# Gates on ScalarE and a later modulation row in a two-block transformer kernel

## The chip, the cores and the metric

The kernel runs on one core of a Trainium2 chip. The core has five engines with queues of their own, which work in order and wait for each other by semaphores: TensorE (PE in the profile; its weight loads are PEld), VectorE (DVE), ScalarE (ACT), GpSimd (POOL) and SyncE (SP), which here only issues transfers. POOL issues transfers too, among them the indirect gathers. The metric is the device time of one execution in microseconds (us); what is compared is the median over several executions.

## The reference, cut to what matters

Two transformer blocks work on 256 tokens of width 1024, all in float32. The first has three attentions, a gated merge and a sparse feed-forward (PEER): for each token, 8 heads pick 16 of 16384 experts each, and an expert is one row `u` and one row `v`.

```python
act = gelu(einsum('chkd,cd->chk', u[ic], hc))      # 128 picks for each token
w = gate * act
out = einsum('chk,chkd->cd', w, v[ic])
```

The second block has two layers, each with a mixer and an expert-choice MoE, on the tokens ("latents") and, in the first layer, on a context of 256 tokens. All norms of it are modulated by rows that come from a condition vector: `mod = silu(c) @ ada_w[i] + ada_b[i]`, cut in six rows of 1024 (shift, scale and gate of the mixer, then of the MoE). The mixer of the first layer is an mLSTM, whose output is normed by head and gated:

```python
y = y * rsqrt(mean(y * y, -1) + EPS)
y = y.reshape(b, t, h * d) * norm_g * sigmoid(o)
```

The mixer of the second layer is a retention.

## The kernel before, in words

The program is one straight line of instructions, written by Python generators that are woven into each other: `drive` runs a main generator and lets side generators go on in proportion to costs that the generators yield. From this the framework makes each engine's order: it simulates the program and places, on each engine, what is ready, with preference by the written order. So the order of an engine's queue isn't exactly the written one, and an edit at one place can move others.

Memory is handed out by hand: an arena `fa` in SBUF, two rings `rt` and `rw` for rounded halves of operands, and eight PSUM banks (`pp`). Weights come as slabs of 1 MB through `Stream`: a dry run records the order of all requests, and in the real run a slab is issued from SP, in that order, as soon as one of some four slots is free. Most weights are split into two parts (high and low, `Units`): ACT copies with rounding, DVE or POOL subtracts; a product is then three matmuls.

First block (0 to some 411 us): projections, attentions and merge, limited by PE. Beside them, `ada_task` (L1222) computes rows of the modulation: for each row it loads the bias, asks for four slabs of `ada_w`, runs 32 small matmuls, and `ada_put` (L1217) adds the bias on DVE and writes the row to DRAM by a transfer from POOL, twice (latents and context). Before, eight rows are done there, two of them of the second layer, and what is left of the last is finished at the start of `peer` (L1276).

`peer` (L1274) norms the tokens, and `mod_cols` (L1512) brings shift and scale of several norms from DRAM as columns: small transfers from POOL, one transpose on PE, copies and fused products on DVE. L1280 does it for the first layer, L1281 for the second layer's mixer.

Then the picks (`picks`, L1332) run as main generator, and beside them, as side work, the query products and routing (`prepare` L1293, `prepare_last`, `route`) and the whole first mixer of the context (`context_task` L1590). Tokens lie on the 128 partitions, in two tiles; for each tile there are 128 picks, one column of the `act` and `gate` arrays each. One pick is: POOL gathers one row of `u` and `v` for each token (1 MB) into one of eight ring buffers; DVE multiplies `u` by the token and sums along the row into a column of `act`; ACT applies Gelu to the column; DVE multiplies it by the gate's column (L1364); ACT makes a diagonal matrix of it by scaling the identity (L1368); PE multiplies this by `v` and adds up in PSUM. A buffer goes back to the ring when PE has read it. The first picks wait for the routing of the first head, which is some 60 instructions of DVE.

The mLSTM: `mlstm_attend` computes head after head, and `mlstm_norm` (L1880), woven beside it, computes the output gates: four products of 512 columns for each of context and latents, each made into a sigmoid by an Exp on ACT, an addition and a reciprocal on DVE (L1888 to L1891). When two heads are there, `norm_pair` (L1906) multiplies them by the inverse root mean square (three Newton steps on DVE) and by the gate. It also serves the retention. Context: beside the picks; latents: after the picks, `mlstm` (L1603).

Then come the first MoE, the retention and the second MoE. The MoEs stream expert weights and are close to what the transfers can do. `block2` (L1536) hands `moe` a function `late` (L1547) that is called when the last group's up-projection is done; it gets room for what the retention needs. The retention starts with norms that use the columns of the second layer's first rows.

Of the kernel before, what the change touches and what calls it, by code (L numbers as in the profile page):

```python
# [14 lines left out]
AF = mybir.ActivationFunctionType  # L15
OP = mybir.AluOpType
AX = mybir.AxisListType

EPS = 1e-6
# [3 lines left out]
RING, BATCH = 8, 1  # L23
# [490 lines left out]
class K:  # L514
# [323 lines left out]
    def block1(self, mem):  # L838
        mT = self.norm_T([m.a for m in mem], self.col("g_mem"), w=1024)
        for m in mem:  # L840
            m.free()
        self.ada_open()
        self.ada = self.ada_task([(0, k) for k in range(6)] + [(1, 0), (1, 1)])
        self.hT = self.norm_T([x.a for x in self.x], self.col("g_mix"))
        self.mkv = self.f(2048)

        mkv = self.mkv.v("p (i f) -> p i f", i=2)
        for s in range(2):
            for i, p in enumerate(self.wide([mT], self.halves("w1", 2 * s))[0]):
                self.act(mkv[:, i, s * 512:(s + 1) * 512], p.a)  # L850
                p.free()
        for b in mT:
            b.free()
        self.dil_buffers()
        self.drive(self.proj_task(), [self.mem_task(), self.sb_task(), self.dil_task()], 0.6)
        self.merge_task()
# [417 lines left out]
    def peer(self):  # L1274
        h2, g = [self.f(1024, True), self.f(1024)], self.bcast_row("ffn")
        self.ada_steps(99)  # L1276
        self.mc = self.f(128, True)
        h2T = self.norm_T([x.a for x in self.x], self.col("g_ffn"), sums=self.sq.a[:, :4], rows=(g, h2))
        self.sq.free(), g.free()
        self.mod_cols(0, [(n, b) for n in range(2) for b in range(2)])  # L1280
        self.mod_cols(1, [(0, 0), (1, 0)])  # L1281
        self.routes = [{"heads": 0, "rows": self.f(128), "gate": self.f(128), "act": self.f(128)} for _ in range(2)]

        for i, x in enumerate(self.x):
            self.nc.sync.dma_start(self.keep[i], x.a)
            x.free()
        self.nc.sync.dma_start(self.keep[2], h2[1].a)
        h2[1].free()
        side = self.chain((0.3 * c for c in self.prepare(h2T)), self.weave(self.context_task(), [self.prepare_last()], 1.5))
        self.drive(self.picks(h2, side), [side], PACE)  # L1290
        self.stream.grow(1)

    def prepare(self, h2T):  # L1293

        self.sc = [self.plain(self.RA) for _ in range(2)]
        sub = self.stream.get(("w1", W1["sub"]))
        self.units.lo = deque([self.nc.gpsimd])
        for s in range(8):
            w = self.wslab(("w1", W1["pq"] + s))
            p = self.slab_T(h2T, w)  # L1300
            q = self.f(512)
            self.act(q.a, p.a)
            p.free()
            self.wfree(w)
            p = self.ps()
            for i in range(2):
                for f in range(2):
                    self.mm(p.a[:, i * 256 + f * 128:i * 256 + f * 128 + 128], q.a[:, f * 256 + i * 128:f * 256 + i * 128 + 128],
                            sub.a[:, (2 * s + f) * 128:(2 * s + f + 1) * 128])
            for i in range(2):  # L1310
                self.act(self.sc[i].a[:, s * 256:(s + 1) * 256], p.a[:, i * 256:(i + 1) * 256])
            p.free(), q.free()
            yield 5200
            if s == 1:
                self.units.lo = deque([None, self.nc.gpsimd])
            if s == 7:
                for b in h2T:
                    b.free()
                sub.free()
                self.stream.shrink(2)  # L1320
                self.units.lo = deque([None])
            if s in (0, 1, 3, 7):
                yield from self.route(0, {0: 0, 1: 1, 3: 2, 7: 4}[s], s + 1)
# [8 lines left out]
    def picks(self, h2, prep):  # L1332


        ident = self.c("ident")
        ring = dg = None
        for i, r in enumerate(self.routes):
            while r["heads"] < 1:
                yield next(prep) * 0
            if ring is None:  # L1340
                ring, dg = deque(self.f(2048, True) for _ in range(RING)), deque(self.f(128, True) for _ in range(4))
            if i:
                self.nc.sync.dma_start(h2[0].a, self.keep[2])
            po = self.ps(2)
            rows, gate, act = (r[n].a for n in ("rows", "gate", "act"))
            for k in range(0, 128, BATCH):
                while r["heads"] * 16 < k + 1:
                    yield next(prep) * 0
                if i and k == 128 - BATCH:

                    ring.popleft().free()
                    self.x = [self.f(1024) for _ in range(2)]
                    self.nc.sync.dma_start(self.x[0].a, self.keep[0])
                got = []
                for j in range(k, k + BATCH):
                    b = ring[0].a
                    ring.rotate(-1)
                    got.append(b)
                    self.nc.gpsimd.indirect_dma_start(b, None, self.t["puv"], bass.IndirectOffsetOnAxis(ap=rows.bitcast(U32)[:, j:j + 1], axis=0))  # L1359
                    self.stt(b[:, :1024], b[:, :1024], 1.0, h2[0].a, OP.mult, OP.mult, accum_out=act[:, j:j + 1])  # L1360
                    yield 2600
                o = act[:, k:k + BATCH]
                self.act(o, o, AF.Gelu)
                self.tt(o, o, gate[:, k:k + BATCH], OP.mult)  # L1364
                for j, b in enumerate(got):
                    d = dg[0].a
                    dg.rotate(-1)
                    self.act(d, ident, AF.Copy, scale=act[:, k + j:k + j + 1])  # L1368
                    for f in range(2):
                        self.mm(po.a[:, f * 512:(f + 1) * 512], d, b[:, 1024 + f * 512:1024 + (f + 1) * 512], k + j == 0, k + j == 127)  # L1370
            if i == 0:
                x = ring[0].a[:, :1024]
                ring.rotate(-1)
            else:
                x = self.x[1].a
            self.nc.sync.dma_start(x, self.keep[i])
            for f in range(2):
                o = x[:, f * 512:(f + 1) * 512]
                self.tt(o, po.a[:, f * 512:(f + 1) * 512], o, OP.add)
            if i == 0:  # L1380
                self.nc.sync.dma_start(self.keep[0], x)
            po.free()
            for n in ("rows", "gate", "act"):
                r[n].free()
        h2[0].free()
        for b in (*ring, *dg):
            b.free()
# [148 lines left out]
    def block2(self, upto):  # L1536
# [10 lines left out]
        def late():  # L1547
            self.sq = self.f(16)
            junk.extend(self.f(256) for _ in range(2))
            self.ret_open()  # L1550

        def squares(n, k):
# [28 lines left out]
        s, r = self.root_mean([x.a for x in self.x], late[1].a[:, :8])  # L1581
# [298 lines left out]
    def mlstm_norm(self, S):  # L1880

        S["yT"] = self.r(2048), self.r(2048)
        for s in range(2):

            b = self.f(1024)
            for i, p in enumerate(self.wide([S["hT"]], self.halves("w2", 8 + 2 * s, S["seg"]))[0]):
                o = b.a[:, i * 512:(i + 1) * 512]
                self.act(o, p.a, AF.Exp, scale=-1.0)  # L1888
                p.free()
                self.ts(o, o, 1.0, OP.add)  # L1890
                self.nc.vector.reciprocal(o, o)  # L1891
            if s == 1:
                for x in S["hT"]:
                    x.free()
            yield 9800
            for j in (4 * s, 4 * s + 2):
                while S.get("heads", 0) < j + 2:
                    yield 5200
                self.norm_pair(S["y"], b, 512, j % 4 * 128, S["ss"].a[:, :16].rearrange("p (i h) -> p i h", i=2)[:, :, j:j + 2], j)
                self.pair_T(S["yT"], [S["y"].a[:, i * 1024:(i + 1) * 1024] for i in range(2)], j, self.col("mlstm_g"))  # L1900
                yield 3000
            b.free()
        for b in (S["ss"], S["y"]):
            b.free()

    def norm_pair(self, y, gate, w, o, ss, j):  # L1906

        t = self.f(16)
        v4 = t.v("p (k i h) -> p k i h", k=4, i=2)
        self.ts(v4[:, 0], ss, 1.0 / 128, OP.mult, EPS, OP.add)  # L1910
        out = t.a[:, 8:12]
        self.root(out, t.a[:, 4:8], t.a[:, :4])
        for i in range(2):
# [557 lines left out]
```

## Time and profile before

| | us |
|---|---|
| median of 3 runs | 2615.86 (2615.13 to 2617.09) |
| the profiled execution | 2619.42 |
| its span, first to last instruction | 2617.7 |
| PE busy | 2265.2 (87%) |
| DVE busy | 1243.2 (47%) |
| ACT busy | 802.9 (31%) |
| POOL busy | 634.4 (24%) |
| read from HBM | 853.63 MB, 327 GB/s over the span |

The span in 40 equal slices of 65 us; each digit is the busy share in tenths, PEclk the granted clock of TensorE in tenths of full speed:

```
PE   7999987799787789777878999999969989878877
DVE  4365448899955676555866122212186461000001
ACT  5564443344622763223643000000042441000000
POOL 3223444344343444332530000000032420000000
PEclk9999988999999899999998999999989999999999
DMA  7467758898999789996446899999966398999997
```

An engine that is seldom busy over the whole span can still set the pace of a stage, and the other way round; so the shares are read stage by stage: slices 0 to 6 are the first block, 6 to 18 the picks, 19 to 21 the latents' mLSTM, 22 to 28 the first MoE, 29 to 33 the retention, and the rest the second MoE. In the profile all ACTIVATEs have one line (L598), as have all two-operand DVE instructions (L605), fused ones (L614) and matmuls (L617), because helpers issue them: they are told apart by shape and by place. A bracket behind an instruction of the timeline is how long its engine had been idle, and who ended that.

### The profile page before, as it was taken

Reading aid. Unit: us, or ns where it says so; the run is one execution under the profiler, and the core shown is the slowest. Engines: PE = TensorE matmul, PEld = TensorE weight load, DVE = VectorE, ACT = ScalarE, POOL = GpSimd, SP = SyncE. Lnnn points to the kernel's source line nnn. Section 1 sums busy time; section 2 is a strip of 40 time slices with the busy share of each in tenths; the row PEclk is TensorE's granted clock in tenths of the full one; section 3 lists DMA queues with packets and bytes.
Section 4 is the critical chain, followed back from the end, with each engine's and each line's share of the span. In section 5 each row is a group of like instructions: output and inputs, shape, how many; then the busy total and the mean of one; then the engine's idle time right before and its main releaser. Section 6 shows DMA issues by size and latency. Waiting matters only on the chain. (4 is left out here: it accounts for less than half of the span.)

```text
span 2617.7 us, 29085 instructions
## 1 busy us (share of the span) xinstructions
PE 2265.2 (87%) x10507; PEld 1276.5 (49%) x10507; DVE 1243.2 (47%) x2943; ACT 802.9 (31%) x1632; POOL 634.4 (24%) x526
## 2 busy tenths in 40 slices
PE   7999987799787789777878999999969989878877
PEld 5867776356332445224666344444459863222223
DVE  4365448899955676555866122212186461000001
ACT  5564443344622763223643000000042441000000
POOL 3223444344343444332530000000032420000000
PEclk9999988999999899999998999999989999999999
DMA  7467758898999789996446899999966398999997
GB/s 295 177 240 258 262 185 324 329 364 333 332 410 419 288 338 394 421 421 251 143 163 266 354 396 420 414 421 421 373 235 240 105 378 334 420 419 420 419 420 319
DMA packets 129534, 858.81 MB, mean 328 GB/s; under 512 B 15342, under 2 KB 15934, under 8 KB 33520
## 3 DMA queue, kind: packets, MB, share of 16 engines
q1 hardware_dynamic: 87120, 573.50, 55.2%
q0 software_dynamic: 42272, 283.47, 27.8%
q8 instruction: 83, 1.36, 0.2%
q14 instruction: 59, 0.48, 0.0%
HBM read 853.63 MB, written 3.28 MB: 327 GB/s over the span
## 5 line engine op out<-in xcount | busy, mean ns | idle before, releaser
L617 PE MATMUL pp<-fa 128*128 128x512 f32 (+10 forms) x4912 | 1289.2, 492 | 220.8 <-ACT fa L598 153.0
L617 PEld LDWEIGHTS pp<-fa 128*128 128x128 f32 (+3 forms) x4912 | 554.0, 159 | 836.5 <-issue 395.3
L617 PE MATMUL pp<-rw,rt 128*128 128x512 f32 (+1 forms) x1896 | 469.6, 401 | 17.4 <-ACT rw L598 5.6
L614 DVE SCALAR_TENSOR_TENSOR fa<-fa 128x1024 f32<-128x1024 f32 (+5 forms) x561 | 406.4, 747 | 109.0 <-DMA fa<-in_puv,fa 104.6
L605 POOL TENSOR_TENSOR rw<-fa,rw 128x1024 fp32r<-128x1024 f32 x84 | 211.5, 2519 | 809.4 <-ACT rw L598 772.0
L617 PEld LDWEIGHTS pp<-rw,rt 128*128 128x128 f32 x1896 | 351.1, 190 | 114.5 <-issue 15.3
L1359 POOL DMA_INDIRECT fa<-in_puv,fa x256 | 278.4, 1087 | 412.5 <-PE pp L617 330.3
L605 DVE TENSOR_TENSOR fa<-pp,fa 128x512 f32<-128x512 f32 (+3 forms) x225 | 128.4, 578 | 525.8 <-PE pp L617 505.2
L598 ACT ACTIVATE fa<-fa 128x1 f32<-128x1 f32 (+9 forms) x601 | 214.1, 375 | 480.7 <-DVE fa L614 351.6
L598 ACT ACTIVATE fa<-pp 128x512 f32<-128x512 f32 (+4 forms) x169 | 93.4, 565 | 710.9 <-PE pp L617 581.3
L598 ACT ACTIVATE rw<-fa 128x1024 fp32r<-128x1024 f32 x208 | 216.4, 1054 | 243.4 <-PE pp L617 164.3
L617 PE MATMUL pp<-rt,fa 128*64 128x512 f32 (+3 forms) x736 | 241.7, 579 | 16.8 <-DMA rt<-in_moe_up 9.7
L605 DVE TENSOR_TENSOR rw<-fa,rw 128x1024 fp32r<-128x1024 f32 x124 | 166.8, 1350 | 171.1 <-ACT rw L598 170.8
L617 PE MATMUL pp<-rt,rw 128*128 128x256 f32 x1632 | 232.2, 301 | 13.8 <-POOL rw L605 4.0
L617 PEld LDWEIGHTS pp<-rt,rw 128*128 128x128 f32 x1632 | 212.6, 200 | 32.7 <-issue 12.1
L617 PE MATMUL pp<-rw,fa 128*64 128x512 f32 (+2 forms) x720 | 207.5, 582 | 13.5 <-DMA rw<-in_moe_down 5.3
L605 DVE TENSOR_TENSOR fa<-fa 128x1 f32<-128x1 f32 (+10 forms) x453 | 124.0, 284 | 81.3 <-ACT fa L598 74.7
L611 DVE TENSOR_SCALAR fa<-pp,fa 128x128 f32<-128x128 f32 (+1 forms) x80 | 36.5, 463 | 247.0 <-PE pp L617 164.1
L598 ACT ACTIVATE fa<-ct,fa 128x128 f32<-128x128 f32 x256 | 101.7, 399 | 103.6 <-DVE fa L605 64.0
L627 PE MATMUL pp<-ct,fa 128*128 128x128 f32 (+2 forms) x441 | 75.6, 308 | 59.7 <-ACT fa L598 27.1
L617 PEld LDWEIGHTS pp<-rt,fa 128*64 128x64 f32 (+1 forms) x736 | 66.1, 125 | 120.7 <-issue 79.3
L617 PEld LDWEIGHTS pp<-rw,fa 128*64 128x64 f32 (+1 forms) x720 | 58.9, 123 | 125.1 <-issue 83.9
(135 smaller groups left out, 961.2 us busy)
## 6 DMA issues: line engine op xcount, KB each, us to landing
fa<-in_w SPq DMA_DIRECT2D x98, 1024.0 KB, 5.3
fa<-in_moe_gate SPq DMA_DIRECT2D x62, 1024.0 KB, 14.1
fa<-in_moe_down SPq DMA_DIRECT2D x59, 1024.0 KB, 16.8
fa<-in_moe_up SPq DMA_DIRECT2D x56, 1024.0 KB, 17.1
fa<-in_ada_w SPq DMA_DIRECT2D x43, 1024.0 KB, 5.0
rw<-in_moe_up SPq DMA_DIRECT2D x36, 1024.0 KB, 16.2
rt<-in_moe_down SPq DMA_DIRECT2D x31, 1024.0 KB, 15.2
rt<-in_moe_up SPq DMA_DIRECT2D x28, 1024.0 KB, 16.2
```

Of the source, the lines that this page charges most:

```text
L598: return self.nc.scalar.activation(out, in_, func, **kw)
L605: (eng or self.nc.vector).tensor_tensor(out, a, b, op=op)
L611: (eng or self.nc.vector).tensor_scalar(out, a, s1, s2, op0=op0, op1=op1, **kw)
L614: self.nc.vector.scalar_tensor_tensor(out, a, s, b, op0=op0, op1=op1, **kw)
L617: self.nc.tensor.matmul(ps, l, r, start=start, stop=stop, skip_group_check=True)
L627: self.nc.tensor.transpose(ps, x, self.c("ident")[:k, :k])
L1359: self.nc.gpsimd.indirect_dma_start(b, None, self.t["puv"], bass.IndirectOffsetOnAxis(ap=rows.bitcast(U32)[:, j:j + 1], axis=0))
```

## The change

There are four edits.

1. Picks: the product of Gelu and gate moves from DVE to ACT, as a copy whose scale is the gate's column.
2. Output gates of the mLSTM: instead of Exp on ACT, addition and reciprocal on DVE, there are Tanh of half the input and an addition of 1 (as the bias of an Identity), both on ACT. That is twice the sigmoid; `norm_pair` gets a factor `by`, 4 here, on the mean square and on EPS, so that the inverse root is halved.
3. The modulation row (1, 1) leaves the first block: `prepare` computes it after the first head's scores, in one go, ahead of the second slab of query weights in the stream.
4. The columns of the second layer's mixer (`mod_cols(1, ...)`) leave `peer` and are taken in `late`, at the end of the first MoE.

```diff
-        self.ada = self.ada_task([(0, k) for k in range(6)] + [(1, 0), (1, 1)])
+        self.ada = self.ada_task([(0, k) for k in range(6)] + [(1, 0)])
...
         self.mod_cols(0, [(n, b) for n in range(2) for b in range(2)])
-        self.mod_cols(1, [(0, 0), (1, 0)])
...
             p.free(), q.free()
+            if s == 0:
+
+                for _ in self.ada_task([(1, 1)]):
+                    pass
             yield 5200
...
-                o = act[:, k:k + BATCH]
-                self.act(o, o, AF.Gelu)
-                self.tt(o, o, gate[:, k:k + BATCH], OP.mult)
+                for j in range(k, k + BATCH):
+                    o = act[:, j:j + 1]
+                    self.act(o, o, AF.Gelu)
+                    self.act(o, o, AF.Copy, scale=gate[:, j:j + 1])
...
             junk.extend(self.f(256) for _ in range(2))
+            self.mod_cols(1, [(0, 0), (1, 0)])
             self.ret_open()
...
-                self.act(o, p.a, AF.Exp, scale=-1.0)
+                self.act(o, p.a, AF.Tanh, scale=0.5)
                 p.free()
-                self.ts(o, o, 1.0, OP.add)
-                self.nc.vector.reciprocal(o, o)
+                self.act(o, o, AF.Identity, bias=1.0)
...
-                self.norm_pair(S["y"], b, 512, j % 4 * 128, ..., j)
+                self.norm_pair(S["y"], b, 512, j % 4 * 128, ..., j, 4.0)
...
-    def norm_pair(self, y, gate, w, o, ss, j):
+    def norm_pair(self, y, gate, w, o, ss, j, by=1.0):
...
-        self.ts(v4[:, 0], ss, 1.0 / 128, OP.mult, EPS, OP.add)
+        self.ts(v4[:, 0], ss, by / 128, OP.mult, by * EPS, OP.add)
```

## Rows read from the trace of the kernel before

**Rows 1.** Stretches of the picks: length, each engine's busy us (instructions), PEclk, DMA share, GB/s.
```profile
430.00:725.00 295.00, 253.06 (x939) 148.21 (x940) 272.13 (x870) 131.64 (x284) 121.03 (x101) 0.94 0.91 343
725.00:850.00 125.00, 97.12 (x218) 37.51 (x216) 67.58 (x163) 30.78 (x101) 47.82 (x50) 0.97 1.01 418
850.00:1050.00 200.00, 166.35 (x552) 92.33 (x552) 136.40 (x342) 112.83 (x258) 86.40 (x80) 0.94 0.89 341
1050.00:1222.00 172.00, 134.56 (x272) 46.14 (x272) 94.73 (x204) 42.08 (x138) 58.40 (x63) 1.00 0.98 409
```

**Rows 2.** Waits of ACT and of PE, 430 to 725: total us, times, longest.
```profile
ACT fa L598 <- DVE fa L605: 41.1, 48, 4.0
...
PE pp L617 <- ACT fa L598: 46.4, 26, 8.7
```

**Rows 3.** DVE groups by form, whole span: count, busy us, mean ns, idle before.
```profile
L605 DVE TENSOR_TENSOR fa<-fa 128x1 f32<-128x1 f32 x256 | 47.1, 186 | 59.0 <-ACT fa L598 58.7 <-issue 0.3
...
L1891 DVE RECIPROCAL fa<-fa 128x512 f32<-128x512 f32 x8 | 26.6, 3340 | 0.1
...
L609 DVE TENSOR_SCALAR fa<-fa 128x512 f32<-128x512 f32 x8 | 5.5, 698 | 0.0
```

**Rows 4.** ACT groups by form, whole span.
```profile
L598 ACT ACT_TABLE_LOAD x88 | 112.9, 1283 | 16.6 <-DVE fa L609 5.6 <-DVE fa L614 5.5 <-PE pp L617 2.5
...
L598 ACT ACTIVATE fa<-fa 128x1 f32<-128x1 f32 x256 | 51.6, 202 | 318.9 <-DVE fa L614 318.4
...
L598 ACT ACTIVATE fa<-fa 128x512 f32<-128x512 f32 x14 | 8.8, 639 | 12.5 <-DVE fa L605 8.6 <-DVE fa L614 2.3 <-DVE fa L1107 1.5
```

**Rows 5.** DVE groups by form in 430 to 725 (first), then 850 to 1050.
```profile
L605 DVE TENSOR_TENSOR fa<-fa 128x1 f32<-128x1 f32 x85 | 17.8, 213 | 9.2 <-ACT fa L598 9.0 <-issue 0.3
...
L605 DVE TENSOR_TENSOR fa<-fa 128x1 f32<-128x1 f32 x60 | 11.5, 196 | 20.1 <-ACT fa L598 20.1
...
L1891 DVE RECIPROCAL fa<-fa 128x512 f32<-128x512 f32 x2 | 6.7, 3348 | 0.0
```

**Rows 6.** Timeline at the change of token tile: start, us, engine, line, instruction.
```profile
846.52 0.99 POOL L1359 DMA_INDIRECT fa<-in_puv,fa  x1 [1.58 <-DVE fa L605]
...
864.36 17.99 PE L617 MATMUL pp<-fa 128*128 128x512 f32 x51 [15.35 <-ACT fa L598]
...
868.18 1.01 POOL L1359 DMA_INDIRECT fa<-in_puv,fa  x1 [2.70 <-PE pp L617]
```

**Rows 7.** Timeline in the latents' mLSTM.
```profile
1363.45 2.90 DVE L609 TENSOR_SCALAR fa<-fa 128x512 f32<-128x512 f32 x2
...
1366.27 6.55 DVE L1891 RECIPROCAL fa<-fa 128x512 f32<-128x512 f32 x2
1372.38 1.40 POOL L605 TENSOR_TENSOR fa<-fa,ct 128x256 f32<-128x256 f32 x2 [5.88 <-DMA fa<-arow]
...
1373.51 14.26 PE L617 MATMUL pp<-fa 128*128 128x129 f32 x92 [10.54 <-DVE fa L614]
```

**Rows 8.** Timeline at the end of the first block: sum and write of a modulation row.
```profile
379.77 0.41 DVE L605 TENSOR_TENSOR fa<-pp,fa 128x256 f32<-128x256 f32 x1
...
383.88 0.59 POOL L1220 DMA_DIRECT2D mods<-fa  x1
```

**Rows 9.** Transfers of modulation weights: engine, operation, count, KB each, us to landing.
```profile
fa<-in_ada_w SPq DMA_DIRECT2D x43, 1024.0 KB, 5.0
```

**Rows 10.** Timeline at the first head's routing.
```profile
405.30 0.24 DVE L1521 COPY fa<-pp 128x16 f32<-128x16 f32 x2
...
411.19 1.04 POOL L1359 DMA_INDIRECT fa<-in_puv,fa  x1 [2.45 <-DVE fa L1494]
```

**Rows 11.** Timeline: the second head's rows are written; its first pick's gather.
```profile
434.17 0.17 DVE L1486 CAST fa<-fa 128x16 uint32<-128x16 f32 x1
...
461.54 1.20 POOL L1359 DMA_INDIRECT fa<-in_puv,fa  x1 [3.58 <-PE pp L617]
```

**Rows 12.** A stretch of the first MoE, columns as in rows 1.
```profile
1450.00:1850.00 400.00, 399.39 (x1748) 168.16 (x1750) 79.96 (x147) 29.30 (x55) 0.00 (x0) 1.00 1.00 411
```

More of the change, by code (lines that the diff above doesn't have):

```diff
@@ L1898, in mlstm_norm @@
                     yield 5200
-                self.norm_pair(S["y"], b, 512, j % 4 * 128, S["ss"].a[:, :16].rearrange("p (i h) -> p i h", i=2)[:, :, j:j + 2], j)
+                self.norm_pair(S["y"], b, 512, j % 4 * 128, S["ss"].a[:, :16].rearrange("p (i h) -> p i h", i=2)[:, :, j:j + 2], j, 4.0)
                 self.pair_T(S["yT"], [S["y"].a[:, i * 1024:(i + 1) * 1024] for i in range(2)], j, self.col("mlstm_g"))
```

## The prediction

> **What bounds the kernel now.** I read the slices of the page first: in their DMA row the transfers are near full from slice 7 on, with dents, the long one (slices 19 to 21) being the mLSTM of the latents. The picks (256 gathers, each feeding one dot product, one gate and two matmuls) run from 411 us to about 1222 us. Then I cut them by stage [rows 1]. Two stretches are paced by transfers: 725 to 850 (share 1.01, 418 GB/s) and 1050 to 1222 (0.98): nothing that DVE, ACT or PE does faster shortens those. Two are not: 430 to 725 has a DMA share of 0.91 with DVE busy 272.1 of 295 us (92%), and 850 to 1050 has 0.89. A share below 1 is time in which the eight ring buffers are full and nobody can start a gather: 0.09 x 295 = 26.6 us and 0.11 x 200 = 22 us. These 48.6 us are all that the picks can give, because the bytes stay the same.
>
> Why the ring is full is told by the waits of 430 to 725 [rows 2]: ACT sat 41.1 us ahead of work that DVE had to release (the scaled identity waits for the gate's product), and PE sat 46.4 us for ACT. So a pick goes DVE (dot product), ACT (Gelu), DVE (x gate), ACT (scaled identity), PE, and the third step stands in DVE's queue behind routing and weight splits.
>
> **The change part by part.**
>
> *Picks' gate product.* Removed: 256 DVE products of one column, 47.1 us [rows 3]; added: 256 ACTIVATEs of the same shape, 0.202 us each [rows 4], 51.7 us. On DVE what counts is the share in the DVE-paced stretch: 85 products, 17.8 us, and up to 9.0 us in which DVE waited for a Gelu to come back [rows 5]. On ACT 85 x 0.202 = 17.2 us are added to 131.6 busy of 295 [rows 1]: it stays about half busy, so I cost it at nothing; if that cover were gone it is rival 3. The pick's chain loses two changes of engine.
>
> *Output gates.* Each of the eight 128x512 blocks loses an addition (0.698 us mean) and a reciprocal (3.340 us) on DVE [rows 3], 4.04 us, and gets one more ACTIVATE, whose nearest row is 0.639 us [rows 4]. Exp becomes Tanh of the same shape, at the same price. Four blocks are the context's and lie among the picks, two of them between 850 and 1050 us [rows 5] and two before 725; four are the latents', behind the picks. Whether Tanh between Gelus still needs table loads is not shown: from none saved to two for each of the four blocks among the picks, 8 x 1.283 us [rows 4] = 10 us of ACT. I take none, since ACT does not pace there. The factor 4 in the norm costs nothing (two constants of one instruction).
>
> Stretch 430 to 725: DVE loses 17.8 + 2 x 4.04 = 25.9 us; the transfers can take up 26.6. Bounds 0 and -26.6. I take half, **-14 us**: the same DVE also carries the rest of the routing, and the mixed weight loads share the queues. Stretch 850 to 1050: bounds 0 and -22. DVE loses 11.5 us of products, waited 20.1 us for Gelus and loses two gates (8.1 us, [rows 3, 5]), but it is not the pacer all through. The clearest place is the change of token tile: a gather went out at 846.52 and the next at 868.18, after PE, which had waited 15.35 us for ACT's scaled identities, went on at 864.36 [rows 6]. I take **-8 us**, half of that wait.
>
> *Latents' mLSTM.* At 1363.45 DVE takes up two additions and two reciprocals, until 1372.8, and PE sits 10.54 us until 1373.51, when DVE can at last weigh the next head's scores [rows 7]. That wait goes; what is late next is the row of the next head, whose copy lands at 1372.38 [rows 7], and the two ACTIVATEs added ahead of it (1.3 us) put it off. Bounds: 0 and 10.5 - 1.3 = -9.2. I take **-5 us**. The first pair of the latents I leave at nothing: other heads' work of PE lies beside it.
>
> *The modulation row.* Before, the row's matmuls run in gaps of PE at the end of the first block; two DVE sums of 0.41 us and two writes from POOL, 0.59 us each, follow [rows 8], and each slab lands 5.0 us after its issue [rows 9]. After, the four slabs come between the first and the second slab of the query weights in SP's queue, and the sums and writes beside the first head's routing, ahead of the first gathers on POOL. PE has room there. Bounds: the routing gets 0.8 us longer and the gathers start 1.2 us later (2.0), up to the whole load added to the picks' transfers, 4.19 MB at the 418 GB/s of a full stretch [rows 1], 10 us, where no idle transfer is left; below, -3 if the first slab of query weights, now earlier in the queue, brings the first head forward. Before the first gather the queries' slabs wait for free slots more than for transfers, so I take most of it as hidden: **+1.5 us**. The columns' part leaves the first head's routing (two copies in 0.24 us, [rows 10], and two fused products of the same width, taken alike): **-0.5 us**. The second head's rows must be there at pick 16, issued at 461.54, and were written at 434.17 [rows 11]: 27 us of slack cover a later second slab.
>
> *The columns at the end of the first MoE.* Two small reads from POOL, one transpose, four small DVE instructions. POOL is idle from 1450 to 1850 [rows 12] and the columns are wanted only by the norm behind the MoE. On PE, which is busy 399.4 of 400 us there, the transpose waits for the reads; if it stands too early in PE's queue, expert matmuls behind it wait for one landing, 5.0 us [rows 9]. Bounds 0 and +5, taken 0.
>
> Sum: -14 - 8 - 5 + 1.5 - 0.5 = **-26 us**. The profiled execution took 2619.42 us (span 2617.7), 3.6 above the median of the runs, 2615.86; from the median this is **2590 us**.
>
> **The rivals.**
>
> 1. *The ring does not follow.* PE, at a mean granted clock of 0.94 in 430 to 725 [rows 1], that is, part of it at the lower level of 1.2 GHz, or the mixed transfers hold the ring as DVE did. Then only the latents' 5 us and 3 us at the tile change stay: 2608. For it: 0.94 is the lowest clock of the four stretches. Against: PE's own waits are for ACT [rows 2].
> 2. *All of it converts.* Both stretches rise to a share near 1: -26.6 - 22 - 5 + 1 = -53, so 2563. For it: 25.9 us of DVE work removed is close to 26.6. Against: the second stretch has other waits.
> 3. *ScalarE becomes the pacer (slower).* Three ACTIVATEs of each pick in a row stand in one queue with weight splits and table loads. It decides from the point where ACT has no idle time in the two stretches; then the 85 + 60 added ACTIVATEs cost 145 x 0.202 = 29 us and only the latents' 5 us are won: 2640. For it: at the tile change it was ACT that PE waited for [rows 6]. Against: ACT is busy 131.6 of 295 and 112.8 of 200 us [rows 1].
> The Trainium skill, page "ScalarE: Activation LUTs", section "Rules for kernel authors", speaks for this one: it says to add and multiply on VectorE, not on ScalarE. By it the product and the addition are moved the wrong way. This trace agrees on the durations by little (0.186 us on DVE against 0.202 on ACT for one column, [rows 3, 4]), but the engine with the queue is DVE.
> 4. *The row in the way (slower).* The four slabs hold back every later slab of the query weights, no transfer is free and DVE runs dry where it was the pacer: no relief in 430 to 725, +10 us there: 2626. It decides once the second head's rows are over 27 us late [rows 11]. Four slabs of 5.0 us make that unlikely.
>
> **How the numbers follow.** Forecast 0.60 (own range 2575 to 2603), rival 1 0.16, rival 2 0.12, rival 3 0.06, rival 4 0.06. The range 2566 to 2614 leaves out rivals 3 and 4 and half of rival 2, 0.18. A measurement of this kernel tells 0.2% (5.2 us) from no change. Faster: the forecast, rival 2 and two thirds of rival 1, 0.83; slower: rivals 3 and 4 less a little, 0.10; the rest, 0.07, within.
>
> **What would show each step.** Right: no one-column product on DVE; the DMA share of the first DVE-paced stretch up from 0.91, and the 64th to 90th gathers some 14 us earlier; the gap between gathers at the tile change (846.5 to 868.2) shorter; no reciprocal of 128x512, and PE's 10.5 us wait in the latents' last heads gone or halved; the first gather within 3 us of 411. Wrong: ACT busy near 90% in these stretches, or PE waiting for ACT for longer than before; the first gather late; a wait of PE for the modulation's transpose at the end of the first MoE; or the order in which the instructions of picks and side work are laid out changing so much that another engine's queue holds the ring.

## The result, and the profile after

The changed kernel took 2586.66 us (median of 4 runs, 2583.92 to 2588.43) against 2615.49 us (4 runs, 2614.58 to 2617.09): a ratio of 0.9888, 95% interval 0.9871 to 0.9905, or 28.8 us less. A later comparison on another chip gave 0.9905 (0.9889 to 0.9922). The time forecast was 2590.

The profiled execution took 2583.92 us, its span 2582.0. That is the fastest of its four runs, while the profiled one of before (2619.42) was slower than all of its own; so the two traces differ by 35.7 us, more than the medians do.

I cut both traces at events that both have: first and last gather; the start of TensorE's wait of 4.3 to 4.5 us that follows the picks by 17 to 18 us; the start of the same kind of wait at the end of the latents' mLSTM; a point 1.9 us ahead of the first transposes of the hook (`late`) at the end of the first MoE; the start of TensorE's wait of 4.2 us at the end of the retention.

| us | before | after | difference |
|---|---|---|---|
| first gather | 411.2 | 406.3 | -4.8 |
| picks, first to last gather | 795.3 | 766.4 | -28.9 |
| latents' mLSTM | 199.3 | 185.0 | -14.3 |
| first MoE up to the hook | 453.9 | 455.8 | +1.9 |
| rest of the MoE and the retention | 277.5 | 291.9 | +14.4 |
| second MoE to the end | 462.3 | 459.5 | -2.8 |

(The missing 1.1 us lies between the last gather and the latents.) So 49 us were gained before the first MoE, and 14 were given back in the retention, a stage that the prediction did not mention.

The four stretches of the picks after the change, as in [rows 1]:

```profile
430.00:725.00 295.00, 256.11 (x950) 148.19 (x949) 261.78 (x782) 168.68 (x387) 138.28 (x112) 0.97 0.93 363
725.00:850.00 125.00, 96.00 (x219) 37.66 (x219) 66.05 (x135) 54.90 (x168) 45.94 (x49) 0.95 0.96 392
850.00:1050.00 200.00, 177.16 (x552) 91.57 (x552) 122.53 (x268) 106.32 (x294) 82.11 (x81) 0.98 0.96 387
1050.00:1222.00 172.00, 136.18 (x422) 63.00 (x420) 92.36 (x165) 69.24 (x195) 57.54 (x61) 0.99 0.82 339
```

In the first stretch the DMA share rose only from 0.91 to 0.93, but the rate from 343 to 363 GB/s; in the third from 0.89 to 0.96, and from 341 to 387. (The last stretch now ends behind the picks, hence its 0.82.) ACT is busy 168.7 of 295 us, 57% where I had expected half, and is far from full.

The waits of ACT and of TensorE in the first stretch, as in [rows 2], and then ACT's groups over the whole span, as in [rows 4]:

```profile
ACT fa L598 <- DVE fa L614: 98.5, 65, 6.2
PE pp L617 <- ACT fa L598: 36.2, 24, 5.2
ACT fa L598 <- DVE fa L605: 4.1, 1, 4.1
```

```profile
L598 ACT ACTIVATE fa<-fa 128x1 f32<-128x1 f32 x512 | 127.0, 248 | 326.2 <-DVE fa L614 315.0 <-issue 2.6
L598 ACT ACT_TABLE_LOAD x86 | 110.3, 1283 | 17.2 <-DVE fa L609 5.8 <-issue 4.7 <-PE pp L617 3.9
L598 ACT ACTIVATE fa<-fa 128x512 f32<-128x512 f32 x22 | 13.8, 631 | 8.2 <-DVE fa L605 4.4 <-DVE fa L614 2.2 <-DVE fa L1107 1.5
```

ACT's wait for the gate's product went from 41.1 to 4.1 us, though ACT does more. TensorE's wait for ACT, 46.4 before and 36.2 after, tells nothing: three other kernels with the product on VectorE (the experiments with Tanh for all gates, with Tanh for the latents, and with row and columns alone) have 30.3 to 38.9 us there. The 256 added one-column ACTIVATEs cost 127.0 - 51.6 = 75.4 us, not 0.202 us each but 0.294; the 256 others stay at 0.202. The eight added blocks are there at 0.631 us. Table loads: 86 instead of 88.

The change of token tile, as in [rows 6]:

```profile
826.59 0.98 POOL L1362 DMA_INDIRECT fa<-in_puv,fa  x1 [3.43 <-DVE fa L614]
831.80 6.70 PE L617 MATMUL pp<-fa 128*128 128x256 f32 x11 [2.11 <-DVE rt L614]
837.49 1.96 POOL L1362 DMA_INDIRECT fa<-in_puv,fa  x1 [9.92 <-DVE fa L614]
```

The gap between the two gathers is 10.9 us instead of 21.7, and TensorE's 15.35 us wait for ACT is gone.

The latents, where [rows 7] has the two reciprocals:

```profile
1333.41 2.87 ACT L598 ACTIVATE fa<-fa 128x256 f32<-128x256 f32 x8 [2.00 <-DMA fa<-arow]
1334.35 0.69 DVE L614 SCALAR_TENSOR_TENSOR fa<-pp,fa 128x512 f32<-128x512 f32 x1 [1.88 <-ACT fa L598]
1335.10 1.15 PEld L617 LDWEIGHTS pp<-fa 128*128 128x128 f32 x5 [5.13 <-DVE fa L614]
1335.10 1.23 PE L617 MATMUL pp<-fa 128*128 128x129 f32 x4 [4.94 <-DVE fa L614]
```

TensorE's wait is 4.94 us instead of 10.54. What ends it is the chain from the row of the next head (its copy lands, ACT takes the Exps, DVE weights the scores), which the prediction had named as next. So this wait gave 5.6 us, close to the 5 that were forecast; the stage gave more.

The start of the retention (four engines; SPq is SyncE's queue of transfers):

```profile
1890.71 1.98 PE L617 MATMUL pp<-fa 128*128 128x256 f32 x8
1891.83 0.69 DVE L605 TENSOR_TENSOR fa<-fa 128x512 f32<-128x512 f32 x1 [4.91 <-PE pp L617]
...
1896.22 9.21 DVE L614 SCALAR_TENSOR_TENSOR fa<-fa 128x1024 f32<-128x1024 f32 x7
1897.54 0.33 SPq L581 DMA_DIRECT2D fa<-in_ada_w  x1
1900.18 0.33 SPq L581 DMA_DIRECT2D fa<-in_w  x1
...
1905.06 2.00 ACT L598 ACTIVATE rw<-fa 128x1024 fp32r<-128x1024 f32 x2 [13.56 <-DMA fa<-in_w]
...
1906.17 0.79 PE L617 MATMUL pp<-rt,rw 128*128 128x256 f32 x2 [13.48 <-ACT rw L598]
```

This is a chain of waits that leads back to TensorE. It stands 13.48 us for the split of a weight slab, which was issued only at 1900.18. Ahead of it in SyncE's queue stood a slab of modulation weights (1897.54), which waited for a slot; by the trace both that slot and the weight slab's own were released by DVE's sums over earlier modulation slabs, and those (1896.22) stood in DVE's queue behind the rotation of the last head group (1891.83), which had waited for TensorE. In the trace of before the same place reads:

```profile
1901.13 2.06 SPq L579 DMA_DIRECT2D fa<-in_ada_w  x2
1908.84 0.33 SPq L581 DMA_DIRECT2D fa<-in_w  x1
1910.83 0.33 SPq L581 DMA_DIRECT2D fa<-in_ada_w  x1
1912.16 1.66 SPq L579 DMA_DIRECT2D fa<-in_w  x2
```

There the third weight slab goes out ahead of the fourth modulation slab, and some slabs go as two halves (L579) into split places of the arena. After the change no slab of the retention is halved and the order is another. The loss lies at this start: the first 400 matmuls after the hook take 89.8 us instead of 75.2, the last 293 up to the end of the retention 58.0 instead of 59.4.

And SyncE's queue at the end of the first block, first after the change:

```profile
330.93 8.62 SPq L581 DMA_DIRECT2D fa<-in_w  x3
349.49 11.21 SPq L581 DMA_DIRECT2D fa<-in_ada_w  x3
```

then before:

```profile
336.12 18.44 SPq L581 DMA_DIRECT2D fa<-in_ada_w  x3
359.68 0.33 SPq L581 DMA_DIRECT2D fa<-in_w  x1
366.30 0.33 SPq L1285 DMA_DIRECT2D keep<-fa  x1
367.51 0.33 SPq L581 DMA_DIRECT2D fa<-in_w  x1
```

Before, the sub-keys and the first slab of the query weights (359.68 and 367.51) stood behind the row's slabs. After, they go out by 339.6, 25 to 28 us earlier, and the row's slabs follow them.

### The profile page after: what moved, and what is told of

Read it like the earlier page. It is cut to its first block, busy times and chain, and to the rows that moved or that the text cites. A ratio compares the mean times of both kernels' runs of the same rounds, so it can differ in the third digit from the quotient of the medians.

```text
span 2582.0 us, 28996 instructions
## 1 busy us (share of the span) xinstructions
PE 2269.8 (88%) x10507; PEld 1272.9 (49%) x10507; DVE 1173.2 (45%) x2672; ACT 880.7 (34%) x1894; POOL 628.4 (24%) x525
## 4 chain that ended last, share of the span: by engine, by line
PE 44%; DMA 19%; DVE 15%; issue 10%; POOL 6%; ACT 5%; another core or an unknown queue 0%; POOLq 0%; DVEq 0%; SPq 0%; ACTq 0%
PE pp L617 43%; DVE fa L614 6%; DMA fa<-in_moe_down 5%; POOL fa L1362 4%; ACT fa L598 3%; DMA fa<-in_moe_up 2%; DMA rw<-in_moe_up 2%; DMA rt<-in_moe_gate 2%; DVE rw L605 2%; DVE fa L605 2%; ACT L598 2%; DMA fa<-in_moe_gate 2%; DMA fa<-in_puv,fa 2%; PE pp L627 1%; DMA fa<-arow 1%
## 5 line engine op out<-in xcount | busy, mean ns | idle before, releaser
L617 PE MATMUL pp<-fa 128*128 128x512 f32 (+8 forms) x4976 | 1306.5, 489 | 188.7 <-ACT fa L598 129.4
L614 DVE SCALAR_TENSOR_TENSOR fa<-fa 128x1024 f32<-128x1024 f32 (+4 forms) x561 | 402.0, 743 | 165.8 <-DMA fa<-in_puv,fa 159.7
L598 ACT ACTIVATE fa<-fa 128x1 f32<-128x1 f32 (+8 forms) x865 | 292.5, 354 | 484.0 <-DVE fa L614 349.9
L1362 POOL DMA_INDIRECT fa<-in_puv,fa x256 | 284.0, 1109 | 424.1 <-PE pp L617 324.8
L605 POOL TENSOR_TENSOR rw<-fa,rw 128x1024 fp32r<-128x1024 f32 x83 | 205.3, 2475 | 331.7 <-ACT rw L598 313.0
L617 PE MATMUL pp<-rt,fa 128*64 128x512 f32 (+3 forms) x704 | 231.7, 577 | 9.8 <-DMA rt<-in_moe_up 4.7
L617 PE MATMUL pp<-rw,fa 128*64 128x512 f32 (+2 forms) x688 | 180.4, 583 | 12.6 <-DMA rw<-in_moe_down 5.1
L627 PE MATMUL pp<-ct,fa 128*128 128x128 f32 (+3 forms) x441 | 73.1, 302 | 51.7 <-ACT fa L598 22.2
L598 ACT ACTIVATE fa<-pp,fa 128x128 f32<-128x128 f32 (+3 forms) x80 | 35.8, 462 | 210.9 <-PE pp L617 146.0
```

The source lines that it names most:

```text
L598: return self.nc.scalar.activation(out, in_, func, **kw)
L605: (eng or self.nc.vector).tensor_tensor(out, a, b, op=op)
L614: self.nc.vector.scalar_tensor_tensor(out, a, s, b, op0=op0, op1=op1, **kw)
L617: self.nc.tensor.matmul(ps, l, r, start=start, stop=stop, skip_group_check=True)
L627: self.nc.tensor.transpose(ps, x, self.c("ident")[:k, :k])
```

## The experiments

All times are compared with the kernel before on the same chip; "ratio" is to it, with its 95% interval, and a gain in us is the ratio's share of that chip's time. "Theory 1" and the rivals are those of each expectation.

**The product alone** on the kernel before:

```
-  self.tt(o, o, gate[:, k:k + BATCH], OP.mult)
+  self.act(o, o, AF.Copy, scale=gate[:, j:j + 1])
```

> Only the picks' product on ScalarE. Theory 1 (VectorE paced 430 to 725 us): the last gather goes out 10 to 20 us before the old 1206, the latents' 10.5 us wait of TensorE stays, nothing after it moves: 2597 to 2606 us. Rival 'ScalarE becomes the pacer': no earlier last gather, 2612 us or more. Rival 'the product was hidden and all of the gain was the gates': within 4 us of 2615.5.

Measured 2595.39 us against 2612.27, ratio 0.9931 (0.9918 to 0.9945): -18 us of this chip's time. The last gather went out at 1189.3, 17 us earlier than in the trace of before and 11 earlier than in that of Tanh for the latents alone, whose picks are those of before (1200.3); the latents took 198.2 us and the retention 277.8, as before. Theory 1 holds; by the middle of the intervals the product is the largest part.

**Tanh gates alone**, all eight blocks (Exp, addition and reciprocal become Tanh of half and Identity plus one; factor 4 in the norm):

> Only the output gates by Tanh, all eight blocks. Theory 1: the picks' last gather 6 to 12 us earlier (four blocks of 4.04 us on VectorE and what they hold up), the latents' mLSTM 9 to 14 us shorter, so 2591 to 2601 us. Rival 'the next row of decay weights lands late anyway': the latents gain under 4 us, 2602 to 2610 us.

Measured 2599.71 us, ratio 0.9953 (0.9939 to 0.9966): -12 us. The latents took 189.2 us instead of 199.3, as theory 1 has it. The last gather went out at 1197.9, 8.5 us earlier; but with unchanged picks it has been at 1200.3 too, so what the context's blocks give can't be told from that scatter.

**Row and columns alone**, gates as before:

> Only the modulation row beside the first head's routing and its columns at the end of the first MoE. Theory 1: the first gather is 4 to 5 us earlier and the picks keep it, but the memory for the weight slabs is laid out in another way from then on, the order of loads in the retention changes with it and TensorE waits there for a slab (13 us at its start in the changed kernel): 2620 to 2628 us. Rival 'the loss in the retention comes from the gates': the gather's 5 us stay, 2609 to 2613 us.

Measured 2608.50 us, ratio 0.9991 (0.9981 to 1.0002): no clear difference. I had expected 2620 to 2628; the time is that of the rival (2609 to 2613), but the rival's reason is not there, since the loss in the retention came without the gates: TensorE waits 13.5 us at the retention's start, and the stage takes 285.6 us instead of 277.5, a loss of 8 and not the full change's 14. And the picks took 783.2 us, 7 to 12 less than with the row in its old place (790.1 and 795.3), and 10 of these lie between the 128th and the 192nd gather; I have not traced them to an instruction.

**The gates alone**, both edits, row and columns as before:

> Both edits of the gates, the modulation row and its columns as before. Theory 1 (the row's move costs the retention about 14 us): the retention takes 275 us as before instead of 290, the first gather is at 411 again, and the whole is faster than the full change: 2573 to 2582 us. Rival 'the loss comes with the earlier arrival, whatever the edits': the retention takes 290 us here too, 2588 to 2594 us.

Measured 2579.28 us, ratio 0.9876 (0.9860 to 0.9892). The retention took 276.6 us, the first gather went out at 409.9. So the loss in the retention comes with the row and the columns and not with the earlier arrival. Against the full change (0.9888 and 0.9905) the intervals overlap: what the move of row and columns wins early it loses late, and on balance no worth of it is shown. The two gate edits add up: 0.9931 and 0.9953 give 0.9884.

**A product put back beside the full change**, on a gate column that was used eight picks ago:

```
+  if j >= 8:
+      self.tt(gate[:, j - 8:j - 7], gate[:, j - 8:j - 7], gate[:, j - 8:j - 7], OP.mult)
```

> The full change with a product of one column put back on VectorE for each pick from the ninth of each tile on, off the chain: it overwrites a gate column that was used eight picks earlier, and nothing waits for it. Theory 1 (VectorE's own load paced 430 to 725): about 80 x 0.19 = 15 us come back there, the last gather goes out 7 to 14 us later than 1173, 2593 to 2600 us by the times of the full change's first runs. Rival 'it was the two changes of engine in each pick's chain': within 4 us of the full change's 2586.7, last gather within 3 us of 1173.

Measured 2593.22 us, ratio 0.9934 (0.9922 to 0.9945); last gather at 1181.4. Theory 1's number, but not as clean as I wrote: I had not seen that the product itself would wait for ACT's read of the gates. In 430 to 725 it was busy for 14.3 us and waited for 20.2:

```profile
L605 DVE TENSOR_TENSOR fa<-fa 128x1 f32<-128x1 f32 x84 | 14.3, 172 | 20.6 <-ACT fa L598 20.2
```

The next kernel takes the wait away.

**A product that waits for no other engine**, beside the full change:

```
+  self.tt(self.mc.a[:, 112:113], got[j - k][:, :1], got[j - k][:, 1:2], OP.mult)
```

> The full change with one more VectorE product of one column for each pick that waits for no other engine: it reads two elements of the pick's product row, which VectorE has just written, and writes a column that nobody reads. It separates what the product that waited for ScalarE (20.2 us of waiting in 430 to 725 in the run before) mixed: load and waiting. Theory 1a (the load of VectorE's queue alone, 85 x 0.17 to 0.19 = 15 us there): last gather 6 to 12 us later than the full change's 1173 to 1176, ratio 0.992 to 0.995. Theory 1b (what held VectorE was its waiting for each Gelu behind which other work stood, the product's own time being small): last gather within 4 us of the full change's, ratio 0.988 to 0.991. Rival 'neither: the removed hand-overs of the pick's chain': ratio 0.988 to 0.991 as well, but then the earlier run's 0.9934 has no explanation.

Measured 2594.20 us, ratio 0.9936 (0.9922 to 0.9950). The product's group in the same stretch, and the waits of ACT and TensorE there:

```profile
L605 DVE TENSOR_TENSOR fa<-fa 128x1 f32<-128x1 f32 x83 | 13.4, 161 | 0.7
```

```profile
ACT fa L598 <- DVE fa L614: 94.6, 55, 6.4
PE pp L617 <- ACT fa L598: 42.9, 29, 5.3
ACT fa L598 <- DVE fa L605: 4.7, 1, 4.7
```

13.4 us of load without a wait are enough. (TensorE's 42.9 us lie within what kernels with the product on VectorE have, 30.3 to 46.4, and tell nothing here.) The 88th gather goes out 304.8 us after the first, and 304.5 with the product of the run before, against 293.5, 296.0 and 294.5 in the three traces of the full change's picks (first profile, repeat, and the even slabs below): 8.5 to 11.3 us later. The last gather goes out at 1180.9, 5 to 8 us later than in the full change's two traces; the picks take 775.1 and 773.8 us against 763.7 to 768.1, and the rate of the transfers in 430 to 725 is 349 and 354 GB/s against 362 to 364. That is theory 1a. The granted clock of TensorE there was 0.94 before, 0.97 after and 0.95 and 0.96 with a product put back; what part of the gain is the clock's was not separated. Against the full change's two ratios the load costs 0.3 to 0.5%, 8 to 12 of the product's 18 us; these were measured on different chips, and how much of the rest is due to the removed hand-overs is not shown. The loss isn't spread evenly: the first 64 picks took 227.6 us instead of 204.8, the next 64 only 176.8 instead of 189.5.

**Tanh for the latents alone:**

> Tanh gates for the latents' four blocks alone, the context's with reciprocal as before. Theory 1: picks as before, the stretch of the latents' mLSTM from 199 to some 190 us, so 9 to 10 us less than before: ratio 0.996 to 0.997. Rival 'the context's blocks carry the gain of the gates': under 5 us less than before, ratio 0.998 or more.

Measured 2601.53 us against 2609.52, ratio 0.9966 (0.9953 to 0.9978), -9 us; the latents took 190.0 us. Theory 1 holds. What all eight blocks give more (0.9953 against 0.9966) is not clear of the intervals.

**Gates and columns**, the row in the first block as before:

> Both edits of the gates and the columns at the end of the first MoE; the modulation row stays in the first block. Theory 1 (the row's move alone changes how the slabs' memory is laid out): loads of half slabs as before, retention 276 us, time within 4 us of the kernel with the gates alone, ratio 0.986 to 0.989. Rival 'the columns in the hook at the end of the MoE cost the retention its 14 us': retention 284 to 292 us, ratio 0.991 or more.

Measured 2590.09 us, ratio 0.9922 (0.9910 to 0.9935), 0.46% above the gates alone, and the retention took 284.5 us. Theory 1's time failed, and both numbers are the rival's; but the rival's cause is not this one. The loads are halved as before and there is no 13 us wait, and up to 2060 us the retention runs like the one without the columns' move. The loss is at its end, where the last heads and the gates of the retention are laid out in another order: the last 293 matmuls take 66.2 us, with the gates alone 59.4. In the full change they take 58.0 and in its repeat 57.9, so these 7 us are no part of the 14 that the full change loses. ACT's table loads and TensorE's waits there, first with the gates alone, 2040 to 2113:

```profile
L598 ACT ACT_TABLE_LOAD x3 | 3.8, 1283 | 0.1
...
PE pp L617 <- ACT fa L598: 0.8, 1, 0.8
```

and then with the columns moved, 2048 to 2127:

```profile
L598 ACT ACT_TABLE_LOAD x5 | 6.4, 1283 | 0.1
...
PE pp L617 <- ACT fa L598: 3.9, 4, 1.7
```

The two added table loads alone can't be the reason: over the whole retention there are 7 here, 5 with the gates alone, and 7 in the full change too, whose end is not longer. So a few small instructions that were moved to a place where POOL was idle cost some 7 us in this kernel, over 200 us later. That it is the order of the other instructions is read from the trace; I made no kernel with the old order by hand.

**The full change with the modulation's slabs spread evenly:** one behind each of the first eight weight slabs of the retention, and the other eight at its last two places (`late(2)` becomes `late(1)`).

> The full change, with the modulation's slabs spread evenly over the retention's projections: one behind each of the first eight weight slabs instead of two, the other eight behind the last two. Theory 1 (the 13.5 us wait at the retention's start is for a weight slab queued behind two modulation slabs on SyncE): the wait falls below 4 us and the retention to 276 to 282 us, the whole to a ratio of 0.983 to 0.986. Rival 'the slab slots are too few there, in any order': the wait turns up elsewhere, retention 288 to 295 us, ratio 0.988 or more.

Measured 2559.07 us, ratio 0.9806 (0.9793 to 0.9819): the best of all kernels here, 50 us under before, and better than theory 1 had it (0.983 to 0.986). The retention took 271.7 us instead of 291.9, and at its start:

```profile
1876.89 0.79 PE L617 MATMUL pp<-rt,rw 128*128 128x256 f32 x2 [1.25 <-DVE rt L605]
1877.48 2.76 PE L627 MATMUL pp<-ct,fa 128*128 128x128 f32 x12
1878.03 14.99 SPq L581 DMA_DIRECT2D fa<-in_w  x2
1879.89 12.78 PE L617 MATMUL pp<-rt,rw 128*128 128x256 f32 x99
1892.51 1.02 PE L617 MATMUL pp<-fa 128*128 128x256 f32 x4
```

The next weight slabs now go out at 1878.03 and by 1893, with no modulation slab between them, and TensorE runs on.

**The full change again, and the gates with even slabs**, on one chip:

> The full change once more, beside the next kernel on one chip. Every theory: ratio 0.987 to 0.991 to the kernel before.

Measured 2589.66 us against 2614.36, ratio 0.9905 (0.9889 to 0.9922). First gather 407.8, latents 188.8, retention 293.0 with a wait of 13.4: the stages repeat, but for 4 us of the latents: 185.0 in the first profile, 186.2 to 188.9 in the four other traces with both gates' edits and the row moved.

> Both edits of the gates and the modulation's slabs spread evenly in the retention; the modulation row and its columns stay where they were before. Theory 1 (the even spreading only mends what the row's move spoiled): the retention stays near 276 us, ratio 0.986 to 0.989, and the full change with even rows (0.981) stays the best, because the row's move brings the first gather, the latents and the second MoE forward by 4, 1 to 5 and 3 us. Rival 'the even spreading is worth 15 to 20 us by itself and the row's move nothing': retention 256 to 262 us, ratio 0.979 to 0.982.

Measured 2578.16 us, ratio 0.9863 (0.9844 to 0.9882), the retention 273.5 us. Theory 1: without the row's move the even spreading gives only 3 us there. Only with both does the kernel reach 0.9806; the move of row and columns is worth some 15 us as soon as the retention does not pay for it.

## Why the prediction was right, and where it was not

The sum was right: -26 us forecast, -28.8 measured. Its terms were right in their mechanism, with one exception, and several were wrong in size.

*VectorE paces 430 to 725.* Right, and shown by the product alone and by the load put back. Whether the -14 was too small is not clear: from the first gather to the 88th (counted from 0) it was 313.1 us before, 293.5 after and 296.0 in the repeat, so -17 to -19.6; but the kernel with Tanh for the latents alone, whose picks are those of before, has 308.6, and against it the gain is 12.6 to 15.1. The bound was wrong. I took 26.6 us as what the transfers could take up, from a share of 0.91; the rate of 343 GB/s against 418 in a full stretch would have left 18%, 53 us. The share of busy time hides how slow the transfers are while they are busy.

*ACT's extra work costs nothing.* Right, although each added ACTIVATE took 0.294 us and not 0.202; rival 3 is out. The Trainium skill, page "ScalarE: Activation LUTs", section "Rules for kernel authors", would leave additions and products to VectorE. The trace agrees on the instruction, 0.186 us on VectorE against 0.294 on ACT; the time does not follow it, since the product alone gave 0.9931 where VectorE's queue is the pacer.

*850 to 1050, -8.* From the 128th to the 192nd gather 224.5 became 211.2 (212.8 in the repeat), so -12 to -13. The place was right: the gap at the tile change shrank by 10.8 us, and the product alone gives 215.7. I had halved the 15.35 us wait; it went altogether. But the parts don't add up here: row and columns alone give 214.8, and both gate edits without them 206.2 to 209.3, shorter than in the full change. Why is not shown.

*The latents, -5.* Mechanism right, size wrong: -9 alone, -10.5 in the repeat and -14.3 in the first profile, against my own bound of -9.2. TensorE's waits for DVE's weighted scores fell from 18.0 to 9.6 us over this stage. I counted one wait and left the first pair of blocks at nothing.

*The modulation row, +1.5.* This step failed, twice. For the gathers its sign was wrong: in the seven traces with the row in its old place the first gather is at 411.0 on average, in the six with the row moved (the full change twice among them) at 407.1. The lower bound of -3 had named the reason (the first query slab comes earlier), and I let the added instructions outweigh it. And I followed the move only up to the picks, so the retention stood at nothing. Its slabs, and the two small buffers that are now taken and given back later, change where later slabs lie in memory; with that the order of SyncE's queue in the retention changed, for +14 us. The even spreading shows that the order was the cause of the loss; that the place in memory was the cause of the order is read from the halves in the queue, and wasn't tried by itself. Nor was the row's move without the columns': it is needed for the loss (with the columns moved alone the loads stay halved and the wait is absent), but that it is enough is not shown.

*The columns, 0.* Nothing is lost in the first MoE: 452.2 us with the columns moved and the row not, and no wait for their transpose. In the full change nothing is lost by them at the end of the retention either (58.0 us for the last 293 matmuls, 59.4 before). The 7 us that they cost there with the gates alone came under my last warning, that the order in which instructions are laid out may change, to which I had given no price.

So in the traces 52 us of gain, where I had counted 27.5 and a loss of 1.5, met 16 of loss that I had not foreseen, and the total came out beside the forecast. That closeness is luck: two errors went against each other. Of the rivals, 1 and 4 are out with 3; the picks' 28.9 us lie between the 22 of the forecast and the 48.6 of rival 2, nearer to the forecast.

## What to carry to other kernels

When one engine paces a stage in which transfers are not full, moving even small instructions off its queue can pay, as long as the engine that takes them has idle time there: 13.4 us of small products put back on VectorE cost 8.5 to 11.3 us of that stage. Where a queue's order is made by a planner, a moved load is to be followed to the end of the program: look at each queue of loads behind it for a slab that has to wait for a slot and stands ahead of one that the next product needs. And compare stages, not totals: here the total agreed with the forecast while a 20 us fault lay in it that one number in the order of loads could mend.

## What the runs showed that I had not expected

A one-column ACTIVATE that multiplies by a column took 0.294 us on average beside a Gelu of 0.202 us, dearer than the VectorE product of 0.186 us that it replaced, and the kernel was still 18 us faster. Whole slabs of 1 MB in the second MoE instead of halves go with 459.2 to 459.8 us there in all six traces with the row moved, against 461.1 to 462.8 in the seven others.
